# Norm additions and token sums moved from GpSimd to VectorE, first weights issued by SyncE, three g tiles in the first FFN

## The chip, the cores and the metric

The kernel runs on one core of a Trainium2 chip. The metric is the device time of one execution in microseconds. Engines go by the names of the profile: PE (TensorE matmul), PEld (its weight load), DVE (VectorE), ACT (ScalarE), POOL (GpSimd) and SP (SyncE, which here only issues DMA).

## The reference

Two transformer blocks on 1024 tokens of width 1024, one after the other, all in float32. Cut to the feed-forward parts, which the change touches:

```python
# first block
x = x + gt_m * rms_norm(y, g_post_mix)          # y: output of the first mixer
h = rms_norm(x, g_pre_ffn) * (1.0 + sc_f) + sh_f
up = dwconv3(h @ w_up, conv_w, conv_b)           # depthwise, width 3, over tokens
gate, val = jnp.split(up, 2, axis=-1)
y = (jax.nn.gelu(gate) * val) @ w_down
x = x + gt_f * rms_norm(y, g_post_ffn)
# second block
x = layernorm(A * x + 0.5 * swiglu(x, ffn1_w1, ffn1_w3, ffn1_w2), ln1_g, ln1_b)
x = layernorm(A * x + mixer(x), ln2_g, ln2_b)
x = layernorm(A * x + 0.5 * swiglu(x, ffn2_w1, ffn2_w3, ffn2_w2), ln3_g, ln3_b)
# swiglu(x, w1, w3, w2) = (silu(x @ w1) * (x @ w3)) @ w2, inner width 2816
```

## The kernel before

The stages follow each other: first mixer (it ends with `mixer1_out`), first FFN (`ffn1`), first `swiglu`, second mixer, second `swiglu`, and the last layer norm whose rows go to `out`. Each of the three FFNs has an up stage (`up`) and a down stage (`down`); of the time line, ffn1's up stage begins behind 517 us, its down tail ends near 1255, the first swiglu's up stage begins near 1297, the second's near 2502.

**Products.** A float32 product is made of three matmuls with operands split into a high and a low part: `split` (L103) lets ACT copy the high part (L87) and DVE subtract it from the source (L106); `mm3` (L108) issues high x high (L111), high x low (L112), low x high (L113). For the weights the names are raw (as loaded), wh and wl; for the tokens xh and xl.

**Up stage.** The inner width goes in 22 steps f of 128 columns; each takes the two weight matrices that belong together (gate and value) and the two halves of the tokens as a 2x2 by 2x2 block product, done with seven products P = 1 to 7 in the manner of Strassen, in the order 1, 2, 6, 7, 4, 5, 3, 12 matmuls of 512 columns each. P = 1 and 5 have their low weight part made by POOL (`POOL_LO`), the others by DVE; P = 6 and 4 need sums of weight blocks, made by POOL (L264, T<-raw). A load brings two f (128x8x256, 1 MB, L125). Loads issued by POOL are held in program order by `keep_in_program_order`; those on SP are not. PSUM banks (bA, bB) are added into `acc` tiles by DVE (L92).

**Token sums.** P = 7, 6 and 3 need sums of token blocks: s23 and s4, high and low. `cross_xt` (L208) makes them at the start of an up stage, for two pairs of token tiles in turn: four PE transposes into a PSUM bank per channel tile (L223), scale and shift to `acc` by ACT or DVE (`affine`, L98 and L205), then s4 and the sum for xh on POOL (L228, L231, L237), the two sums for s23 on DVE, and the splits.

**ffn1's glue** (L1675). When the gate's and the value's products are there (h[0], h[1], `acc` 0 and 1), ACT and DVE make the convolution (`conv`: ACT writes u at L1670, DVE adds two shifted terms with L101), ACT the gelu (L1683), DVE the product g * v. g is in `acc` tile 2 for even f and 4 for odd, v in 3 and 5. `left` (L383) then forms, for two f, the seven left operands of the down stage in place in the g tiles and stores them from SP to `gd` (L389): an even f stores half of g, an odd f stores its own g, combines with the even one's and stores that.

**Down stages and norms.** The tokens come in tiles of 128 rows in the order n = 0 to 7. In ffn1 `normed` (L1711) closes a pair of tiles: scale by the rms factor and gate, add the stored rows of the residual x1d (L1724), store to x2r. In the last layer norm, `ln_tail` with `last` (L660 to L679), ACT normalises (L673), then one multiply (L675) and one add (L677) per tile follow, split over POOL and DVE by tile.

**What sets the order.** A tile scheduler orders the instructions of each engine by priority and readiness; engines then run in order and wait by semaphores. `high_priority` raises the weights' preparation. `right` (L409) makes sums of w_down rows for ffn1's down stage during `mixer1_out`; its POOL work and DMAs are held in program order.

Of the kernel before, what the change touches and what calls it, by code (L numbers as in the profile page):

```python
# [13 lines left out]
OP = mybir.AluOpType  # L14
# [6 lines left out]
FF = 2816  # L21
# [17 lines left out]
class Kern:  # L39
# [168 lines left out]
    def cross_xt(self, pair, S23, S4, tmp, scale, bias):  # L208


        nc = self.nc
# [4 lines left out]
        r = lambda a: a.rearrange("p (t c) -> p t c", t=2)  # L216
        kept = lambda k: self.acc[:, o + k % 2, :].rearrange("p (i c) -> p i c", i=2)[:, :,
                                                                                      k // 2 * 256:k // 2 * 256 + 256]
        for k in range(4):
            ps = self.bankB([128, 2, 256])  # L220
            for i in range(2):
                for t in range(2):
                    nc.tensor.transpose(ps[:, i, t * 128:(t + 1) * 128], tiles[:, i, k, t, :], self.ident)  # L223
            hf = tiles[:, :, k]
            self.affine(hf, ps.rearrange("p i (t c) -> p i t c", t=2), k, k + 4, scale, bias, k % 2)
            a = kept(k)
            s4 = tmp[k]
            nc.gpsimd.tensor_tensor(out=r(s4), in0=r(a[:, 1]), in1=hf[:, 1], op=OP.subtract)  # L228
            self.tt(r(a[:, 0]), r(a[:, 0]), hf[:, 0], OP.subtract)
            self.tt(r(a[:, 1]), hf[:, 1], r(a[:, 0]), OP.subtract)  # L230
            nc.gpsimd.tensor_tensor(out=hf[:, 0], in0=hf[:, 0], in1=hf[:, 1], op=OP.add)  # L231
            self.split(S23[0][:, :, k, lc], S23[1][:, :, k, lc], a)
            x = [x[:, k::4, tk].rearrange("p i (t c) -> p i t c", t=2) for x in (self.xh, self.xl)]
            self.split(*x, hf)
        yield
        for k in range(4):
            nc.gpsimd.tensor_tensor(out=tmp[k], in0=tmp[k], in1=kept(k)[:, 0], op=OP.add)  # L237
            self.split(S4[0][:, k, lc], S4[1][:, k, lc], tmp[k])
        yield

    def up(self, pool, loads, h1, glue, scale, bias, gd, during=None, start=None, below=None):
# [112 lines left out]
        tmps = [spare[:, 2 + i // 2, i % 2 * 256:i % 2 * 256 + 256] for i in range(4)]  # L354
# [229 lines left out]
    def swiglu(self, w1, w3, w2, h1, ln, last, base, init, scale=None, bias=None, spill=None, during=None):  # L584
# [16 lines left out]
        with tc.tile_pool(name="up", bufs=1, reuse_waits="tile") as pool:  # L601
            self.up(pool, [lambda f, w=w: self.load_cols(w, f * 128, eng=nc.gpsimd) for w in (w1, w3)], h1, glue,
                    scale, bias, gd, during, below=(w2, td))
# [28 lines left out]
    def ln_tail(self, pool, ln, eps, last, bufs=5, rows=None):  # L632
# [3 lines left out]
        gb = []  # L636
# [1828 lines left out]
```

## Time and profile before

| | us |
|---|---|
| median of 3 runs | 3225.34 |
| lowest, highest | 3224.27, 3226.10 |
| the profiled execution | 3220.59 |
| its span in the trace | 3218.8 |
| mean granted PE clock | 0.953 |

The profile is of one execution. Its page gives the busy time of each engine and the costliest groups; the trace behind it answers for single stretches: busy time and granted clock by window, waits with what ended them, and a time line with every instruction's start, its duration, and in brackets the idle time before it with the releaser. PEclk is the granted clock as a share of full speed.

### The profile page before, as it was taken

The page shows a single profiled execution, that of the slowest core. Times are in us where ns is not written, and L with a number is a line of the kernel's source. Part 1 is how long each engine was busy: PE and PEld are TensorE (multiplying, and loading weights), DVE is VectorE, ACT ScalarE, POOL GpSimd, SP SyncE. Part 2 cuts the span into 40 slices and gives each one's busy share as a digit, 9 for nine tenths or more (in the row PEclk, how much of TensorE's full clock was granted, in tenths as well). Part 3 has the DMA queues.
Part 4 walks back from the last instruction along what each step waited for, and adds up shares of the span by engine and source line. Part 5 has one row for each costly group of instructions (what it writes and reads, how often), then busy time and mean ns, then how long its engine had stood idle before and what let it go on. Part 6 is the DMA issues. An engine that isn't in the chain of part 4 may idle for free. (4 is left out here: it accounts for less than half of the span.)

```text
span 3218.8 us, 38064 instructions
## 1 busy us (share of the span) xinstructions
PE 2932.0 (91%) x13810; PEld 2317.2 (72%) x13810; DVE 2368.8 (74%) x3855; ACT 1249.0 (39%) x2023; POOL 1168.6 (36%) x1001
## 2 busy tenths in 40 slices
PE   6899996799898999699999999977999799999996
PEld 4675565677777887578887888875677677887885
DVE  6982656887878656877776577799857887777567
ACT  5122532433333443323222443557762422222442
POOL 4422267655544002645553001131313655453003
PEclk9899998899999999799999999989999899999998
DMA  6116364222222673344444773110012265444762
GB/s 212 55 34 246 136 199 156 72 87 84 93 85 91 233 229 133 118 161 151 152 159 168 253 246 105 41 34 1 14 68 104 78 237 190 156 160 167 264 213 88
DMA packets 175508, 440.18 MB, mean 137 GB/s; under 512 B 16296, under 2 KB 36040, under 8 KB 175192
## 3 DMA queue, kind: packets, MB, share of 16 engines
q1 hardware_dynamic: 138924, 307.20, 27.4%
q0 software_dynamic: 36032, 130.19, 12.3%
q8 instruction: 109, 1.79, 0.2%
q14 instruction: 79, 0.65, 0.1%
q10 hardware_dynamic: 364, 0.35, 0.0%
HBM read 315.41 MB, written 122.27 MB: 136 GB/s over the span
## 5 line engine op out<-in xcount | busy, mean ns | idle before, releaser
L87 ACT ACTIVATE wh<-raw 128x512 fp32r<-128x512 f32 (+1 forms) x506 | 407.3, 826 | 839.6 <-PE bB L112 207.9
L106 DVE TENSOR_TENSOR wl<-raw,wh 128x1024 fp32r<-128x1024 f32 (+1 forms) x370 | 439.3, 1193 | 245.0 <-ACT wh L87 243.6
L111 PE MATMUL bB<-xh,wh 128*128 128x512 f32 (+1 forms) x860 | 343.3, 399 | 4.7 <-ACT xh L87 4.5
L112 PE MATMUL bB<-xl,wh 128*128 128x512 f32 (+1 forms) x860 | 340.3, 396 | 4.2 <-DVE xl L106 4.2
L113 PE MATMUL bB<-xh,wl 128*128 128x512 f32 (+1 forms) x860 | 339.5, 395 | 0.7 <-DVE wl L106 0.6
L92 DVE TENSOR_TENSOR acc<-acc 128x512 f32<-128x512 f32 (+2 forms) x306 | 306.7, 1015 | 19.6 <-DMA gdln_g<-acc 9.5
L106 POOL TENSOR_TENSOR wl<-raw,wh 128x512 fp32r<-128x512 f32 (+1 forms) x136 | 220.7, 1625 | 220.1 <-ACT wh L87 210.3
L111 PE MATMUL bA<-xh,wh 128*128 128x512 f32 (+1 forms) x508 | 211.4, 417 | 90.0 <-DVE acc L92 53.3
L264 POOL TENSOR_TENSOR T<-raw 128x512 f32<-128x512 f32 x132 | 200.1, 1516 | 182.9 <-DMA raw<-in_ffn_w 96.4
L92 DVE TENSOR_TENSOR acc<-bA,acc 128x512 f32<-128x512 f32 x226 | 150.4, 685 | 127.4 <-PE bA L113 127.1
L92 DVE TENSOR_TENSOR acc<-bB,acc 128x512 f32<-128x512 f32 x260 | 178.1, 686 | 69.2 <-PE bB L113 58.7
L264 POOL TENSOR_TENSOR T<-raw,T 128x512 f32<-128x512 f32 x66 | 106.8, 1619 | 309.4 <-DVE wl L106 307.0
L112 PE MATMUL bA<-xl,wh 128*128 128x512 f32 (+1 forms) x508 | 208.2, 411 | 1.0 <-DVE xl L106 1.0
L113 PE MATMUL bA<-xh,wl 128*128 128x512 f32 (+1 forms) x508 | 207.8, 409 | 0.2 <-DVE wl L106 0.2
L111 PEld LDWEIGHTS bB<-xh,wh 128*128 128x128 f32 x860 | 164.0, 191 | 46.8 <-ACT xh L87 6.0
L112 PEld LDWEIGHTS bB<-xl,wh 128*128 128x128 f32 x860 | 163.6, 190 | 44.6 <-DVE xl L106 5.9
L87 ACT ACTIVATE wh<-T 128x512 fp32r<-128x512 f32 x198 | 118.2, 624 | 191.9 <-PE bA L112 88.9
L113 PEld LDWEIGHTS bB<-xh,wl 128*128 128x128 f32 x860 | 163.4, 190 | 39.5 <-DVE wl L106 1.3
L111 PEld LDWEIGHTS bA<-xh,wh 128*128 128x128 f32 x508 | 101.5, 200 | 122.6 <-ACT wh L87 73.2
L101 DVE SCALAR_TENSOR_TENSOR acc<-acc,cw 128x1023 f32<-128x1023 f32 x88 | 138.6, 1576 | 62.2 <-ACT acc L1670 61.7
L111 PE MATMUL bA<-wh 128*128 128x512 f32 x432 | 170.5, 395 | 12.8 <-DVE acc L92 12.8
L112 PE MATMUL bA<-wl,wh 128*128 128x512 f32 x432 | 169.7, 393 | 0.0
(527 smaller groups left out, 7401.9 us busy)
## 6 DMA issues: line engine op xcount, KB each, us to landing
raw<-in_ffn_w POOLq DMA_DIRECT2D x44, 1024.0 KB, 6.1
raw<-gdln_g SPq DMA_DIRECT2D x70, 512.0 KB, 4.1
raw<-in_w_up POOLq DMA_DIRECT2D x22, 1024.0 KB, 6.2
tq<-in_ffn_w SPq DMA_DIRECT2D x44, 512.0 KB, 4.9
tdln_g<-tq SPq DMA_DIRECT2D x44, 512.0 KB, 2.6
gdln_g<-acc SPq DMA_DIRECT2D x44, 512.0 KB, 2.6
raw<-tdln_g SPq DMA_DIRECT2D x40, 512.0 KB, 5.0
raw<-gd SPq DMA_DIRECT2D x35, 512.0 KB, 4.0
```

Of the source, the lines that this page charges most:

```text
L87: self.nc.scalar.activation(out=out, in_=in_, func=AF.Copy)
L92: self.nc.vector.tensor_tensor(out=out, in0=a, in1=b, op=op)
L101: self.nc.vector.scalar_tensor_tensor(out=out, in0=a, scalar=s, in1=b, op0=op0, op1=op1)
L106: (eng or self.nc.vector).tensor_tensor(out=lo, in0=src, in1=hi.bitcast(F32), op=OP.subtract)
L111: mm(out, lhsT=wh, rhs=xh, start=start, stop=False)
L112: mm(out, lhsT=wh, rhs=xl, start=False, stop=False)
L113: mm(out, lhsT=wl, rhs=xh, start=False, stop=stop)
L264: sub = lambda o, a, b: nc.gpsimd.tensor_tensor(out=o, in0=a, in1=b, op=OP.subtract)
```

## The change

- `cross_xt` works on two channel tiles at a time (q = 0, 1). All sums are DVE operations of 512 elements (`self.tt`): ten per cross in place of eight DVE and twelve POOL operations of 256. The splits are grouped by q; the s4 temporaries are two of [128, 2, 256] in place of four of [128, 256].
- The loads of f = 0 in all three up stages are issued by SP (`eng=f and nc.gpsimd` gives 0, so the default) and no longer held in program order.
- In the last layer norm, and in ffn1's `normed`, all multiplies and adds are on DVE.
- In ffn1's glue g takes `acc` tiles 2, 3, 4 in turn by f % 3, and v is always tile 5.

```diff
@@ cross_xt
-        r = lambda a: a.rearrange("p (t c) -> p t c", t=2)
-        kept = lambda k: self.acc[:, o + k % 2, :].rearrange("p (i c) -> p i c", i=2)[:, :,
-                                                                                      k // 2 * 256:k // 2 * 256 + 256]
-        for k in range(4):
-            ps = self.bankB([128, 2, 256])
+        kept = self.acc[:, o:o + 2, :].rearrange("p j (i q c) -> p q j i c", i=2, q=2)
+        r = lambda a: a.rearrange("p j (t c) -> p j t c", t=2)
+        for q in range(2):
+            ks = slice(2 * q, 2 * q + 2)
+            for k in range(2 * q, 2 * q + 2):
+                ps = self.bankB([128, 2, 256])
+                for i in range(2):
+                    for t in range(2):
+                        nc.tensor.transpose(ps[:, i, t * 128:(t + 1) * 128], tiles[:, i, k, t, :], self.ident)
+                self.affine(tiles[:, :, k], ps.rearrange("p i (t c) -> p i t c", t=2), k, k + 4, scale, bias, k % 2)
+            a = kept[:, q]
+            h0, h1 = tiles[:, 0, ks], tiles[:, 1, ks]
+            self.tt(r(tmp[q]), r(a[:, :, 1]), h1, OP.subtract)
+            self.tt(r(a[:, :, 0]), r(a[:, :, 0]), h0, OP.subtract)
+            self.tt(r(a[:, :, 1]), h1, r(a[:, :, 0]), OP.subtract)
+            self.tt(h0, h0, h1, OP.add)
...
-            nc.gpsimd.tensor_tensor(out=r(s4), in0=r(a[:, 1]), in1=hf[:, 1], op=OP.subtract)
-            self.tt(r(a[:, 0]), r(a[:, 0]), hf[:, 0], OP.subtract)
-            self.tt(r(a[:, 1]), hf[:, 1], r(a[:, 0]), OP.subtract)
-            nc.gpsimd.tensor_tensor(out=hf[:, 0], in0=hf[:, 0], in1=hf[:, 1], op=OP.add)
...
-        for k in range(4):
-            nc.gpsimd.tensor_tensor(out=tmp[k], in0=tmp[k], in1=kept(k)[:, 0], op=OP.add)
-            self.split(S4[0][:, k, lc], S4[1][:, k, lc], tmp[k])
+        for q in range(2):
+            ks = slice(2 * q, 2 * q + 2)
+            self.tt(tmp[q], tmp[q], kept[:, q, :, 0], OP.add)
+            self.split(S4[0][:, ks, lc], S4[1][:, ks, lc], tmp[q])
@@ swiglu, and the same in ffn1
-            self.up(pool, [lambda f, w=w: self.load_cols(w, f * 128, eng=nc.gpsimd) for w in (w1, w3)], h1, glue,
+            self.up(pool, [lambda f, w=w: self.load_cols(w, f * 128, eng=f and nc.gpsimd) for w in (w1, w3)], h1, glue,
@@ ln_tail, last
-                    (nc.gpsimd if i - t + n in (0,2,5) else nc.vector).tensor_tensor(out=o[:, a], in0=o[:, a], in1=gb[0][:, a],
-                                                                      op=OP.mult)
-                    (nc.vector if m else nc.gpsimd).tensor_tensor(out=o[:, a], in0=o[:, a], in1=gb[1][:, a], op=OP.add)
+                    self.tt(o[:, a], o[:, a], gb[0][:, a], OP.mult)
+                    self.tt(o[:, a], o[:, a], gb[1][:, a], OP.add)
@@ ffn1, glue
-                o = 2 + f % 2 * 2
-                g, v = acc[:, o, :], acc[:, o + 1, :]
+                g, v = acc[:, 2 + f % 3, :], acc[:, 5, :]
@@ ffn1, normed
-                    (nc.vector if n > 5 else nc.gpsimd).tensor_tensor(out=a, in0=a, in1=x, op=OP.add)
+                    self.tt(a, a, x, OP.add)
```

The order of the instructions changes at the three starts of an up stage and in the two tails. (Behind the diff's lines in `cross_xt`, `ln_tail` and `ffn1` the line numbers of the changed kernel are 3, 2 and 1 higher.)

SP between the loads of w_out and ffn1, before (raw are the staging tiles, t the rows of the residual):

```order
L1600 DMA raw<-in_w_out 64x1024 x4
L1642 DMA x1d<-t_3070 128x1024
L1642 DMA x1d<-t_3157 128x1024
L1642 DMA x1d<-t_3265 128x1024
L1642 DMA x1d<-t_3352 128x1024
```

And SP at the same place in the changed kernel:

```order
L1602 DMA raw<-in_w_out 64x1024 x4
L125 DMA raw<-in_w_up 128x8x256 x2
L1644 DMA x1d<-t_3070 128x1024
L1644 DMA x1d<-t_3157 128x1024
L1644 DMA x1d<-t_3265 128x1024
```

The two first loads of w_up stand ahead of all eight stores of x1d.

POOL from the last sums of w_down rows (tq, td) to the first sums of weight blocks (T), before:

```order
L432 TENSOR_TENSOR tq<-tq 128x256 x4
L434 DMA td<-tq 128x2x256 x2
L125 DMA raw<-in_w_up 128x8x256 x2
L106 TENSOR_TENSOR wl<-raw,wh 128x512 x2
L228 TENSOR_TENSOR raw<-acc 128x256 x2
L231 TENSOR_TENSOR acc<-acc 128x2x128
L237 TENSOR_TENSOR raw<-raw,acc 128x256
L231 TENSOR_TENSOR acc<-acc 128x2x128
L237 TENSOR_TENSOR raw<-raw,acc 128x256
L228 TENSOR_TENSOR raw<-acc 128x256 x2
```

POOL there in the changed kernel:

```order
L435 TENSOR_TENSOR tq<-tq 128x256 x4
L437 DMA td<-tq 128x2x256 x2
L106 TENSOR_TENSOR wl<-raw,wh 128x512 x2
L267 TENSOR_TENSOR T<-raw 128x512
L267 TENSOR_TENSOR raw<-raw 128x4x128
L267 TENSOR_TENSOR T<-raw 128x512
L106 TENSOR_TENSOR wl<-raw,wh 128x512
```

The loads and the token sums are gone; the two low parts still stand behind the sums of w_down rows, and the weight sums follow at once. PE's order is the same in both: two matmuls of the first product, twelve transposes of token tiles, then the L113 that reads the first wl.

DVE in the last tail, ahead of the four additions of PSUM banks that let PE go on, before (rs_t and rstd belong to the rsqrt, t are output rows, lnr the gain or bias):

```order
L106 TENSOR_TENSOR wl<-raw,wh 128x1024
L92 TENSOR_TENSOR rs_t<-rstd 128x2
L92 TENSOR_TENSOR rs_t<-rs_t,rs_h 128x2
L101 SCALAR_TENSOR_TENSOR rstd<-rs_t,rstd 128x2
L101 SCALAR_TENSOR_TENSOR lnb<-mv,rstd 128x1
L675 TENSOR_TENSOR t_22743<-t_22743,lnr 128x1024
L101 SCALAR_TENSOR_TENSOR lnb<-mv,rstd 128x1
L106 TENSOR_TENSOR wl<-raw,wh 128x1024
L675 TENSOR_TENSOR t_22851<-t_22851,lnr 128x1024
L92 TENSOR_TENSOR acc<-bA,acc 128x512 x4
```

And DVE there in the changed kernel:

```order
L106 TENSOR_TENSOR wl<-raw,wh 128x1024
L92 TENSOR_TENSOR rs_t<-rstd 128x2
L92 TENSOR_TENSOR t_22652<-t_22652,lnr 128x1024
L92 TENSOR_TENSOR t_22659<-t_22659,lnr 128x1024
L92 TENSOR_TENSOR t_22652<-t_22652,lnr 128x1024
L92 TENSOR_TENSOR t_22659<-t_22659,lnr 128x1024
L92 TENSOR_TENSOR rs_t<-rs_t,rs_h 128x2
L92 TENSOR_TENSOR acc<-bA,acc 128x512 x4
```

Four operations on output rows now stand ahead of the four additions; one weight split, the end of the rsqrt and the two lnb have moved behind them. In ffn1's up stage the order on DVE is the same in both from about f = 4 on; there only the tiles of g and v differ.

## Rows read from the trace of the kernel before

**Rows 1.** Page, first part: busy us (share) xinstructions of each engine.

```profile
PE 2932.0 (91%) x13810; PEld 2317.2 (72%) x13810; DVE 2368.8 (74%) x3855; ACT 1249.0 (39%) x2023; POOL 1168.6 (36%) x1001
```

**Rows 2.** Stretches: us, busy of PE, PEld, DVE, ACT, POOL; PEclk, DMA, GB/s.

```profile
535.70:600.00 64.30, 37.73 (x177) 30.60 (x178) 53.23 (x82) 29.49 (x57) 42.51 (x39) 0.73 0.20 66
600.00:1060.00 460.00, 422.66 (x1738) 336.69 (x1737) 371.25 (x401) 165.54 (x228) 226.52 (x140) 0.96 0.27 94
658.00:662.00 4.00, 3.92 (x17) 3.21 (x18) 3.84 (x5) 1.24 (x1) 3.81 (x4) 1.00 0.61 193
792.00:796.00 4.00, 4.00 (x12) 3.12 (x11) 2.37 (x3) 1.16 (x1) 3.81 (x3) 0.57 0.68 220
836.60:881.20 44.60, 40.87 (x168) 32.55 (x168) 35.75 (x39) 15.71 (x22) 22.58 (x15) 0.96 0.26 89
1297.00:1352.00 55.00, 40.81 (x164) 32.38 (x163) 52.72 (x64) 23.16 (x50) 44.16 (x40) 0.72 0.22 76
1450.00:1900.00 450.00, 448.01 (x1936) 363.22 (x1935) 315.43 (x377) 152.53 (x218) 150.58 (x110) 1.00 0.54 183
2502.00:2560.00 58.00, 41.21 (x198) 34.14 (x197) 57.02 (x81) 27.72 (x53) 40.85 (x37) 0.79 0.23 78
```

**Rows 3.** Waits of PE, 480 to 600: line <- releaser, us, times, longest.

```profile
PE bA L111 <- ACT wh L87: 28.5, 2, 26.5
```

**Rows 4.** Time line at ffn1's start: start, us, instruction, [idle before].

```profile
543.64 0.80 PE L111 MATMUL bA<-xh,wh 128*128 128x512 f32 x1 [26.52 <-ACT wh L87]
...
547.99 0.78 PE L113 MATMUL bA<-xh,wl 128*128 128x512 f32 x1
...
535.72 1.80 POOL L125 DMA_DIRECT2D raw<-in_w_up  x2
...
445.81 72.67 SPq L1642 DMA_DIRECT2D x1d<-t  x7
```

**Rows 5.** Waits of PE and of DVE, 600 to 1060.

```profile
PE bA L111 <- DVE acc L92: 37.3, 11, 4.6
...
DVE acc L101 <- ACT acc L1670: 60.4, 35, 4.0
```

**Rows 6.** Time line of DVE, then ACT, 853 to 893 (two f of ffn1).

```profile
853.28 2.52 DVE L92 TENSOR_TENSOR acc<-acc 128x512 f32<-128x512 f32 x3
...
862.32 2.20 DVE L101 SCALAR_TENSOR_TENSOR acc<-acc,cw 128x1023 f32<-128x1023 f32 x1 [3.56 <-ACT acc L1670]
...
871.15 1.28 DVE L101 SCALAR_TENSOR_TENSOR acc<-acc,cw 128x1023 f32<-128x1023 f32 x1 [1.31 <-ACT acc L1670]
...
875.86 1.21 DVE L92 TENSOR_TENSOR acc<-acc 128x1024 f32<-128x1024 f32 x1
...
861.05 1.24 ACT L1670 ACTIVATE acc<-acc,cw 128x1024 f32<-128x1024 f32 x1 [4.86 <-DMA gd<-acc]
...
890.43 1.24 ACT L1670 ACTIVATE acc<-acc,cw 128x1024 f32<-128x1024 f32 x1
```

**Rows 7.** Groups by form, 546 to 600: xcount, busy, mean ns, idle.

```profile
L228 POOL TENSOR_TENSOR raw<-acc 128x256 f32<-128x256 f32 x8 | 7.9, 995 | 2.2 <-DVE acc L98 2.2
...
L92 DVE TENSOR_TENSOR acc<-acc 128x256 f32<-128x256 f32 x16 | 10.4, 682 | 0.3 <-ACT acc L205 0.3
```

**Rows 8.** Waits of PE: 1225-1296, 1296-1380, 2502-2580, 3140-3219, in this order.

```profile
PE bA L111 <- DVE acc L92: 5.7, 2, 3.9
...
PE bA L111 <- ACT wh L87: 8.0, 1, 8.0
...
PE bA L111 <- ACT wh L87: 4.6, 1, 4.6
...
PE bA L111 <- DVE acc L92: 10.0, 2, 8.9
```

**Rows 9.** Time line of DVE in the last tail.

```profile
3153.12 2.38 DVE L92 TENSOR_TENSOR rs_t<-rstd 128x2 f32<-128x2 f32 x1
...
3166.24 2.47 DVE L92 TENSOR_TENSOR acc<-bA,acc 128x512 f32<-128x512 f32 x4
```

More of the change, by code (lines that the diff above doesn't have):

```diff
@@ L215, in cross_xt @@
         tiles = self.acc[:, 2 * pair:2 * pair + 2, :].rearrange("p t (i k c) -> p i k t c", i=2, k=4)
-        r = lambda a: a.rearrange("p (t c) -> p t c", t=2)
-        kept = lambda k: self.acc[:, o + k % 2, :].rearrange("p (i c) -> p i c", i=2)[:, :,
-                                                                                      k // 2 * 256:k // 2 * 256 + 256]
-        for k in range(4):
-            ps = self.bankB([128, 2, 256])
-            for i in range(2):
[L222 to L227, printed above, removed]
-            nc.gpsimd.tensor_tensor(out=r(s4), in0=r(a[:, 1]), in1=hf[:, 1], op=OP.subtract)
-            self.tt(r(a[:, 0]), r(a[:, 0]), hf[:, 0], OP.subtract)
-            self.tt(r(a[:, 1]), hf[:, 1], r(a[:, 0]), OP.subtract)
-            nc.gpsimd.tensor_tensor(out=hf[:, 0], in0=hf[:, 0], in1=hf[:, 1], op=OP.add)
-            self.split(S23[0][:, :, k, lc], S23[1][:, :, k, lc], a)
-            x = [x[:, k::4, tk].rearrange("p i (t c) -> p i t c", t=2) for x in (self.xh, self.xl)]
-            self.split(*x, hf)
@@ new lines, in cross_xt @@
+        kept = self.acc[:, o:o + 2, :].rearrange("p j (i q c) -> p q j i c", i=2, q=2)
[14 more added lines that the diff above has]
+            self.tt(h0, h0, h1, OP.add)
+            for i in range(2):
+                self.split(S23[0][:, i, ks, lc], S23[1][:, i, ks, lc], a[:, :, i])
+                x = [x[:, 4 * i + 2 * q:4 * i + 2 * q + 2, tk].rearrange("p j (t c) -> p j t c", t=2)
+                     for x in (self.xh, self.xl)]
+                self.split(*x, tiles[:, i, ks])
@@ L353, in up @@
             prep(*seq[s])
-        tmps = [spare[:, 2 + i // 2, i % 2 * 256:i % 2 * 256 + 256] for i in range(4)]
+        tmps = [spare[:, 2 + q, :].rearrange("p (j c) -> p j c", j=2) for q in range(2)]
         cross = [self.cross_xt(2 * (1 - h1) + i, S23, S4, tmps, scale, bias) for i in range(2)]
@@ L1690, in start @@
                 self.copy(cw[0], ps.rearrange("p a b -> p (a b)"))
-            self.up(pool, [lambda f, o=o: self.load_cols(wu, o + f * 128, eng=nc.gpsimd) for o in (0, FF)], 0, glue,
+            self.up(pool, [lambda f, o=o: self.load_cols(wu, o + f * 128, eng=f and nc.gpsimd) for o in (0, FF)], 0, glue,
                     self.gs_f, self.sh_f, gd, start=start)
```

## The prediction

> **What bounds the kernel now.** I read the page's busy shares first, then the table of stretches, then the waits of each stretch, and for each wait the time line around it. The reader is to see that TensorE is the bound and where it is not fed. PE is busy 91% of 3218.8 us, DVE 74%, POOL 36% [rows 1]; so a change that touches only DVE, POOL and SP can pay only where PE waits for them. The table of stretches shows where [rows 2]. In the first swiglu's up stage (1450 to 1900) PE issues 1936 matmuls in 450 us, 0.2324 us each, at granted clock 1.00: nothing to gain. In the up stage of ffn1 (600 to 1060) 1738 matmuls take 460 us; at 0.2324 they would take 404, so 56 us are lost. The waits of PE there are 37.3 us, 11 times, all for a DVE line that adds a PSUM bank into acc [rows 5]. The rest, 0.04 x 460 = 18 us, is the clock (mean 0.96). What the clock does behind a wait is in the rows too: after the 1.33 us wait at 658 the next 4 us stand at 1.00, after the 2.8 us wait at 791 they stand at 0.57, between the two levels of 1.2 and 2.4 GHz [rows 2]. The other losses are the three starts of an up stage (granted clock 0.73, 0.72 and 0.79 [rows 2]) and the two tails, each with waits of its own [rows 3, 8].
>
> **The first weights (SP for POOL).** PE waits 26.5 us before its first ffn1 matmul at 543.64 [rows 3, 4]. The chain behind it: POOL works off the w_down row sums that are pinned ahead, issues the two 1 MB loads at 535.72, they land about 6 us later, ACT converts, PE starts [rows 4]. SP in the changed kernel has the two loads behind the w_out loads and ahead of all x1d stores; the first x1d store goes out at 445.81 [rows 4], so the weights lie ready some 70 us before 517, when mixer1_out's last matmul ends. What is queued behind them on SP are the x1d stores, whose reader is the down stage 700 us later; price nothing. What is late next: the low parts of P = 1 are POOL work (two L106) and still stand behind the row sums. They ran at 542.6 behind the ACT conversion; now they can begin at 535.72, and PE's first L113, which waits for them, moves from 547.99 [rows 4] to about 537.2 (535.72 plus one of 1.48): 10.8 us, the lower bound. But PE's order puts the first twelve token transposes ahead of that L113, so that the cross chain on DVE starts near 523 and not at 546. The waits behind the start (6.8 us at 569.4 for s23l, 3.5 at 582.4 for acc, and six smaller ones of 6 us together, by the same view as [rows 3]) lie on that chain. If all of them go, 10.8 + 16.3 = 27 us is the upper bound. By the chain s23l is done near 550, about when the 48 early matmuls end (537.2 + 48 x 0.2324 = 548.4 and some clock), against 569.4 before: 18 us, and a little of the later ones. **I take 20.** For the first swiglu the same edit works on the 8.0 us wait at 1296.5 [rows 8]: POOL issues its loads at 1286.3, behind two norm adds, and PE has been idle for most of the time when they land. For the second swiglu the loads were already in time; the edit is worth nothing there.
>
> **Token sums (cross_xt) on DVE.** Per cross 12 POOL operations of 128x256, 1.0 us each, go [rows 7]; two crosses at each of three starts make 72. DVE had 8 of 256 elements at 0.68 [rows 7], 5.5 us, and gets 10 of 512. A 512 operation of this kind costs 0.84 in the steady stage (three in 2.52 [rows 6]), so 8.4 us per cross: 3 more than before. The ends are 6.1, at half of the 1.21 us that 1024 elements take [rows 6], and 10, were each as slow as the POOL operation that it replaces. Against that, DVE work next to POOL is stretched: an operation on 128x2, 0.16 us where POOL is idle, took 2.38 beside a POOL add [rows 9]. Over the first start I count 20 us of stretch (each operation against the shortest of its form) in 51 us of DVE, with 38 us of POOL work; removing 23 us of that POOL work should take 11 to 12 of the stretch away. Net about 5 us less DVE per start, and POOL reaches its weight sums (L264) earlier by the 12 us that the cross sums took. In the first start this is inside the 20. In the swiglu1 start PE waits 8.0 [rows 8], then 4.9, 3.4 and 7.4 at 1315, 1331 and 1373, and runs 55 us at 0.72 [rows 2]. I take all of the 8.0, a third of the other three (5) and 2 of clock: **15** (8 to 22). In swiglu2 the waits are 4.6 [rows 8], 4.6, 4.3, 2.4 and 2.4 at clock 0.79 [rows 2]; a third of them and 1 of clock: **7** (0 to 12).
>
> **Three g tiles.** In the period of two f from 836.6 to 881.2 PE issues 168 matmuls (39.0 us at 0.2324) in 44.6 us, DVE is busy 35.75 [rows 2]. At 853.28 DVE makes the three combinations of an odd f, SP stores them; at 861.05 ACT starts the convolution of the next even f after 4.86 us of waiting for a store gd<-acc, since it writes the same tile; DVE stands 3.56 us behind it at 862.32 [rows 6]; its evictions come late, and PE waits 3.7 us at the end of the period. DVE waits for that convolution 60.4 us in 35 times, 4.0 at the longest [rows 5]. With three tiles the store has a whole f more. What stays of the 3.56 is the usual 1.31 that DVE waits for ACT's convolution [rows 6]: 2.25 direct. The rest follows only if PE's leftover wait is short enough for the clock to stay, as behind the 1.33 us wait [rows 2]. DVE is late next: 35.75 busy + its own waits for ACT (four, 0.71 and 3 x 1.31) and for a store (0.36) = 40.75 per two f, above PE's 39.0. So 44.6 (the mean distance of the waits is 45.4) goes to about 40.8, 4.2 less, ten times in the stage: **42**. Bounds: 2.25 x 10 = 23, and all 56. The v tile becomes a single one; its product ends at 877.07 and the next v convolution starts at 890.43 [rows 6], 13 us apart, so it costs nothing.
>
> **Norm tails.** In ffn1's down tail four POOL adds of 2.4 to 3.4 us stretch DVE and PE waits 5.7 us, 3.9 of it at once [rows 8]. DVE gets them at 1.2 each; with the clock behind it, **5** (0 to 8). In the final tail PE waits 8.9 of 10.0 us at 3167.66 [rows 8] for four evictions that DVE reaches at 3166.24 [rows 9]. From 3153.12 on DVE spends 13.1 us ahead of them, of which rs_t 2.38, rstd 2.26, wl 2.53 and a multiply 3.36 are held by POOL. The new order has a 0.16, four of 1.2 and another 0.16 there: 5.2 us, so the evictions run by 3158.4, when PE's bank is ready. 7.5, and 2 of clock. Behind PE's end three small operations held for 5.6 us lose the hold, two or three adds of 1.2 come in, and the last one should end some 3.5 sooner. **13** (6 to 16).
>
> **Sum.** 20 + 42 + 5 + 15 + 7 + 13 = 102 on the profiled execution's 3220.59; it stands 4.75 below the median of the runs, 3225.34, so I carry the difference over to the median: 3225.34 - 102 = **3123**. All lower bounds (10.8 + 8 + 0 + 23 + 0 + 6 = 48) give 3177, all upper ones (27 + 22 + 12 + 56 + 8 + 16 = 141) 3084.
>
> **Rivals.** (a) *The g tiles give only the direct part.* DVE, at 40.75 of a possible 44.6, has a second wait behind the first, PE's leftover stays over 2 us and the clock falls each time. For: DVE has 371 us of work in 460 [rows 2], ordered by hand-set priorities. Against: 1.3 us waits keep the clock. Gain 23 for 42: 3142. (b) *DVE holds the starts.* The ten moved sums per cross meet POOL's weight sums, which now begin at the same time, and each waits for a whole one, 1.3 to 1.7 us. POOL has 42.5 - 23 = 19 us left in the first start [rows 2, 7], which caps the price at 19 per start. The 128x2 operation that took 2.38 [rows 9], as long as a POOL add of 1024 elements in that tail (2.40), speaks for such a hold; that the cross sums on DVE already ran beside POOL before, at 0.68 each [rows 7], speaks against a full one. Held to the cap it eats the 15 and 7 and half of the 20: 3155. The Trainium skill, page "SBUF — State Buffer", section "SBUF: two separate sides", has a rule for it: VectorE and GpSimd share a pair of ports under an exclusive lock, and a VectorE operation with two SBUF inputs that meets a GpSimd operation is held until that one ends. By that rule the trace agrees for the 128x2 operation, and all the moved sums are of the held kind, which would make (b) the outcome; the forecast goes by the 0.84 of the rows. (c) *The upper end*: PE runs through ffn1 at 0.2324 and the first start loses every wait: 102 + 14 + 7 = 123, 3102 or less. (d) *Slower*: the single v tile. If ACT's v convolution had to wait for the product of the f before, DVE, ACT and PE would run in turn in each of 22 f. With the 42 gone, 60 us of other gains remain, so it decides from 60 / 22 = 2.7 us per f; at 4 us per f the time is 3225 - 60 + 88 = 3253. The 13 us of slack speak against it. (e) *It doesn't do what it says*: SP's loads wait for staging tiles until the end of mixer1_out and hold the x1d stores; then the first start gives nothing more than POOL's relief (8): 3135, still inside (a).
>
> **How the numbers follow.** Forecast, 3103 to 3141: 0.62, (e) within it. (a), 3142 to 3155: 0.13. (b) 0.09. (c) 0.11. (d) 0.03. Everything cancels: 0.02. The range 3092 to 3165 leaves out (d), the cancelled case, a part of (b) and the far end of (c). A measurement of this kernel can tell about 0.2%, 6.5 us, from no change; faster by more 0.95, within it 0.02, slower by more 0.03.
>
> **What would show it.** In the profile after: no ACT wait for gd<-acc in ffn1 and PE waits there under 2 us with the clock at 1.00; if the waits stay over 2.5 us with the clock falling, the g step is wrong as (a). The first L113 of ffn1 near 537 and the wait for s23l gone; the wait before the first matmul of swiglu1 gone. DVE operations on 128x2 at 0.16 in the tails. 128x512 sums above 1.3 us in the starts would show (b); an ACT wait for a DVE product in front of each v convolution would show (d).

## The result and the profile after

The changed kernel takes 3133.1 us (median of 4 runs, 3131.9 to 3135.9), the kernel before 3224.8 in the runs beside it: 0.9723 of the time, 95% interval 0.9703 to 0.9743, that is 89 us less by this ratio and 92 by the medians. The forecast was 3123. The profiled execution after took 3134.06 us with a span of 3132.3; against the profiled one before (span 3218.8) 86.5 us less. What follows is read on that pair.

Where they went can be read from the start of the same matmul in both traces (below: "by the same matmuls"). A difference with a minus means that the changed kernel is ahead there.

| place (time before, us) | difference there | gained in the stretch | forecast |
|---|---|---|---|
| end of mixer1_out (516) | +3.5 | | |
| behind ffn1's start (600) | -11.5 | 15.0 | 20 |
| ffn1 up, 600 to 700 | -10.1 | -1.4 | } 42 |
| ffn1 up, 700 to 1060 | -43.2 | 33.1 | } |
| ffn1's down tail (1256) | -49.8 | 6.6 | 5 |
| swiglu1's start (1400) | -66.3 | 16.5 | 15 |
| second mixer (2500) | -65.4 | -0.9 | |
| swiglu2's start (2700) | -71.2 | 5.8 | 7 |
| last tail (3175) | -80.7 | 9.5 | 9.5 |
| end of the span (3218.8) | -86.5 | 5.8 | 3.5 |

The 3.5 us ahead of the first changed instruction are no work of the change: 2.2 of them stand already at 400, before SP's new loads at 421, and the run of the third experiment, the same kernel up to there, stands at -1.7 at 516; the fifth, there the kernel before, stands at +3.3. So the stretches of the change gained 90.0, where the forecast had 102.

The page's first part, after: PE is busy 15 us less than before [rows 1] with the same 13810 matmuls, as its mean granted clock is 0.966 and was 0.953, and has 93% of a shorter span; POOL lost 115 us and 94 instructions.

```profile
PE 2917.2 (93%) x13810; PEld 2306.4 (74%) x13810; DVE 2333.0 (74%) x3871; ACT 1247.9 (40%) x2011; POOL 1053.4 (34%) x907
```

The stretches of after (columns as in [rows 2]): ffn1's up stage, three places of it, one period of two f, two places outside it, the starts of swiglu1 and swiglu2, and the last tail.

```profile
588.50:1016.70 428.20, 410.20 (x1739) 327.09 (x1738) 373.95 (x399) 166.91 (x227) 221.11 (x138) 0.99 0.29 100
...
649.50:653.50 4.00, 4.00 (x11) 3.15 (x12) 3.29 (x4) 1.72 (x2) 3.00 (x3) 0.62 0.28 38
732.30:736.30 4.00, 4.00 (x17) 3.25 (x18) 3.28 (x4) 1.25 (x1) 3.90 (x4) 1.00 0.66 224
935.30:939.30 4.00, 4.00 (x18) 3.23 (x19) 3.28 (x4) 1.24 (x1) 3.81 (x4) 1.00 0.69 226
...
691.50:732.30 40.80, 39.47 (x169) 31.52 (x169) 35.62 (x39) 15.92 (x22) 22.03 (x15) 1.00 0.28 97
...
522.50:526.50 4.00, 4.00 (x20) 3.29 (x21) 3.79 (x12) 3.99 (x8) 3.06 (x5) 0.71 0.51 161
1658.70:1662.70 4.00, 4.00 (x18) 3.23 (x19) 2.69 (x4) 1.16 (x2) 3.29 (x4) 1.00 0.33 131
...
1240.00:1296.00 56.00, 42.45 (x192) 34.71 (x193) 49.95 (x80) 25.37 (x48) 23.44 (x16) 0.85 0.30 104
...
2436.00:2494.00 58.00, 47.32 (x238) 39.56 (x237) 50.99 (x87) 29.31 (x54) 26.03 (x17) 0.88 0.31 100
3069.00:3101.00 32.00, 31.53 (x139) 25.81 (x138) 27.83 (x60) 11.96 (x11) 0.00 (x0) 1.00 0.39 141
```

The matmuls of ffn1's up stage that took 460 us (1738 records, [rows 2]) take 428 (1739). A period of two f is 40.8 us and DVE has the same 35.6 us of work in it as before (35.75 in 44.6). In the last tail PE is fed to the end of the down products: it is busy 31.5 of 32 us. The starts of swiglu1 and swiglu2 stand at a clock of 0.85 and 0.88 (0.72 and 0.79 before [rows 2]). In the middle of swiglu1 the difference stays at -66.3 for 500 us. In ffn1's up stage the clock follows the waits as it did before: behind 2.70 us of waiting at 649.5 the next 4 us stand at 0.62, behind 1.32 at 732.3 and 1.70 at 935.2 at 1.00.

The waits of PE and of DVE in ffn1's up stage of after, 590 to 1020:

```profile
PE bA L111 <- DVE acc L92: 15.9, 10, 5.0
...
DVE acc L101 <- ACT acc L1672: 40.2, 36, 1.3
```

Against [rows 5]: DVE's wait for ACT's convolution fell from 60.4 to 40.2, the longest from 4.0 to 1.3, the usual length that the prediction set aside. ACT has no wait for a store of gd left. Of PE's 15.9 us, 5.0 are at 602 and 2.7 at 649; from 690 on none is over 1.7.

### The profile page after: what moved, and what is told of

Its sections match the earlier page's. It is cut to its first block, busy times and chain, and to the rows that moved or that the text cites. A ratio compares the mean times of both kernels' runs of the same rounds, so it can differ in the third digit from the quotient of the medians.

```text
span 3132.3 us, 37952 instructions
## 1 busy us (share of the span) xinstructions
PE 2917.2 (93%) x13810; PEld 2306.4 (74%) x13810; DVE 2333.0 (74%) x3871; ACT 1247.9 (40%) x2011; POOL 1053.4 (34%) x907
## 4 chain that ended last, share of the span: by engine, by line
PE 50%; DVE 12%; ACT 3%; issue 2%; POOL 2%; DMA 2%; SPq 0%; DVEq 0%; POOLq 0%; ACTq 0%
PE bB L112 8%; PE bB L111 8%; PE bB L113 8%; PE bA L111 7%; PE bA L112 6%; PE bA L113 6%; DVE acc L92 3%; DVE wx L2072 1%; PE bB L2268 1%; DVE wl L106 1%; PE bB L2252 1%; DMA raw<-in_ffn_w 1%; POOL T L267 1%; ACT junk L2086 1%; PE bA L2219 1%
## 5 line engine op out<-in xcount | busy, mean ns | idle before, releaser
L106 DVE TENSOR_TENSOR wl<-raw,wh 128x1024 fp32r<-128x1024 f32 (+1 forms) x370 | 427.7, 1161 | 212.4 <-ACT wh L87 211.4
L106 POOL TENSOR_TENSOR wl<-raw,wh 128x512 fp32r<-128x512 f32 (+1 forms) x136 | 227.9, 1680 | 449.8 <-ACT wh L87 426.8
L113 PE MATMUL bB<-xh,wl 128*128 128x512 f32 (+1 forms) x860 | 340.6, 396 | 13.0 <-POOL wl L106 12.3
L92 DVE TENSOR_TENSOR acc<-acc 128x512 f32<-128x512 f32 (+1 forms) x294 | 304.5, 1047 | 15.0 <-DMA gdln_g<-acc 8.4
L113 PE MATMUL bA<-xh,wl 128*128 128x512 f32 (+1 forms) x508 | 203.8, 401 | 0.0
L113 PEld LDWEIGHTS bB<-xh,wl 128*128 128x128 f32 x860 | 164.0, 191 | 52.3 <-POOL wl L106 12.9
L112 PEld LDWEIGHTS bB<-xl,wh 128*128 128x128 f32 x860 | 164.2, 191 | 40.1 <-issue 1.2
L106 DVE TENSOR_TENSOR wl<-T,wh 128x512 fp32r<-128x512 f32 x198 | 149.3, 778 | 28.7 <-ACT wh L87 28.3
L113 PE MATMUL bA<-wh,wl 128*128 128x512 f32 x432 | 168.2, 389 | 0.0
```

The lines of the kernel that those rows point to most:

```text
L92: self.nc.vector.tensor_tensor(out=out, in0=a, in1=b, op=op)
L106: (eng or self.nc.vector).tensor_tensor(out=lo, in0=src, in1=hi.bitcast(F32), op=OP.subtract)
L112: mm(out, lhsT=wh, rhs=xl, start=False, stop=False)
L113: mm(out, lhsT=wl, rhs=xh, start=False, stop=stop)
```

## Experiments

Each was timed beside the kernel before, and the ratio with its 95% interval is to that; the medians are compared with the changed kernel's 3133.1. Stretches by the same matmuls are read on the profiled executions and, but for the fifth experiment, named by the changed kernel's times.

**1. Two g tiles again.**

```diff
-                g, v = acc[:, 2 + f % 3, :], acc[:, 5, :]
+                g, v = acc[:, 2 + f % 2 * 2, :], acc[:, 3 + f % 2 * 2, :]
```

> The changed kernel with g back on two tiles (acc 2 and 4) and v on 3 and 5; all else as changed. Theory: in the changed kernel's trace the period of two f in ffn1 is 40.1 to 41.1 us from 691 on, against 45.4 before, over the 8 periods in which ACT waited for a store of gd. With two tiles the wait returns in all of them: 8 x 4.2 = 33 us, so about 3166 against 3133, PE waits of 3 to 4.6 us each 45 us apart and the clock below 1.00 behind them. Rival: the stage went faster because the starts and the tails left DVE less behind; then the tile itself is worth only the direct part, 2.25 x 8 = 18 us (3151), with waits about 2 us and the clock kept.

3179.3 us, 0.9855 (0.9833 to 0.9878) of before: 46 more by the median, 39.7 by the profiled pair, of which 37.7 lie between 608 and 1017 of ffn1 and nothing elsewhere. The waits in its up stage (PE, ACT, 590 to 1070):

```profile
PE bA L111 <- DVE acc L92: 41.8, 11, 5.1
...
ACT acc L1672 <- DMA gd<-acc: 45.1, 9, 7.5
```

The store's wait is back, PE waits 3.8 to 5.1 us every 45 us from 695 on. The rival, in which the other parts carry the stage, is out.

**2. First loads on POOL again.**

```diff
-eng=f and nc.gpsimd
+eng=nc.gpsimd
```

> The changed kernel with the first loads of all three up stages back on POOL, in program order. Theory: in ffn1 the loads go out behind the row sums near 538 and land near 545, as before; but the second low part on POOL was not done before 540 in the changed kernel either, and the token sums chain ran only behind it, so the loss is only the difference of the two, about 8 us: near 3141. In the first swiglu POOL has no norm adds ahead of the loads any more, so they are in time and the wait before the first matmul does not come back. Rival: the loads on SP carry the whole gain of both starts, 15 + 8 us: near 3156, with the 8 us wait back at the first swiglu.

3147.3 us, 0.9757 (0.9732 to 0.9781): 14 more. By the same matmuls all of it stands at ffn1's start, from -2.3 at 516 to +13.7 at 608; what follows adds up to 3 and loses it again. PE's waits at ffn1's start, 505 to 600, and two places of DVE's time line there:

```profile
PE bA L111 <- ACT wh L87: 30.9, 2, 29.4
...
551.20 0.54 DVE L98 TENSOR_SCALAR acc<-bB,gs_f,sh_f 128x256 f32<-128x256 f32 x1 [0.60 <-ACT acc L205]
...
569.50 1.29 DVE L106 TENSOR_TENSOR s23l<-acc,s23h 128x512 fp32r<-128x512 f32 x2
```

The place is as expected, the 8 us was too little. What it left out: here all of DVE's chain from the token tiles to s23l, 18.3 us, runs behind the first product (551.20 to 569.50). In the changed kernel a first part of it ran from 524.6 to 536.0, and only 10.5 us stood behind the late product (545.98 to 556.47, shown with the sixth experiment). At the first swiglu PE's longest wait before the steady part is 3.5 us, and that start loses 1.4.

**3. Token sums as before.** `cross_xt` and its four temporaries from the kernel before, all else as changed.

> The changed kernel with the token sums as before: per channel tile of 256 elements, twelve of them on POOL. Theory: POOL work beside DVE stretches DVE and delays the weight sums; the three starts lose some 5 (ffn1), 8 (first swiglu) and 5 us (second): near 3150, and the DVE operations of 128x256 in the starts are at 0.6 to 0.7 us each instead of 0.34. Rival: the moved sums are held by POOL's weight sums as long as they save; then it is within 5 us of 3133.

3148.7 us, 0.9763 (0.9742 to 0.9783): 15.6 more. The profiled pair, 16.3 apart, has 7 at ffn1's start (from -5.2 at 516 to +1.8), 5.6 at swiglu1's and 9 at swiglu2's. Groups by form at swiglu1's start, of this kernel (1240 to 1300) and then of the changed one (1235 to 1290):

```profile
L92 DVE TENSOR_TENSOR acc<-acc 128x256 f32<-128x256 f32 x16 | 10.6, 675 | 0.0
L106 DVE TENSOR_TENSOR s23l<-acc,s23h 128x512 fp32r<-128x512 f32 x8 | 9.5, 1218 | 0.0
```

```profile
L92 DVE TENSOR_TENSOR acc<-acc 128x512 f32<-128x512 f32 x12 | 7.9, 676 | 0.0
...
L106 DVE TENSOR_TENSOR s23l<-acc,s23h 128x512 fp32r<-128x512 f32 x8 | 5.4, 675 | 0.0
...
L92 DVE TENSOR_TENSOR raw<-raw,acc 128x512 f32<-128x512 f32 x4 | 4.8, 1217 | 0.0
...
L92 DVE TENSOR_TENSOR raw<-acc 128x512 f32<-128x512 f32 x4 | 2.7, 677 | 0.0
...
L92 DVE TENSOR_TENSOR rs_t<-rs_y 128x2 f32<-128x2 f32 x3 | 0.4, 145 | 0.0
```

Sixteen operations of 256 elements beside POOL's 24 took 10.6 us. The changed kernel has twenty of 512 for all of them: sixteen at 0.68, and four (raw<-raw,acc) at 1.22 in the mean, together 15.4 us. So all of POOL's sums cost DVE 4.8 us in two crosses. DVE gets more than that back in its other work: the same eight s23l splits took 9.5 us and take 5.4, and the operations on 128x2 are at 0.145. Counted as the prediction counts stretch (each operation against the shortest of its form), DVE's stretch in this start is about 24 us here, 22 in the kernel before and 10 in the changed one.

The mean of 1.22 hides two kinds. DVE and POOL of the changed kernel at one of the four:

```profile
1263.12 1.76 DVE L92 TENSOR_TENSOR raw<-raw,acc 128x512 f32<-128x512 f32 x1
...
1262.72 1.61 POOL L267 TENSOR_TENSOR raw<-raw 128x512 f32<-128x512 f32 x1
```

Two of the four met a POOL weight sum and took 1.76 and 1.75, the other two 0.68. Over the three starts, 54 of the 60 moved sums took 0.63 to 0.69; six took 0.97 to 1.77, and each of these ended 0.54 to 0.55 us behind the end of a POOL operation that it met. So the hold of rival (b) of the prediction is there, but few of the moved sums meet it: it costs 4.8 us over the three starts, where (b) had up to 19 per start. The rival of this experiment, in which the hold eats the gain, is out.

**4. Tails on POOL again.** The four lines of `ln_tail` and `normed` as before.

> The changed kernel with the multiplies and adds of the last layer norm and the adds of ffn1's norm split over POOL and DVE as before. Theory: the last tail loses its 16 us and ffn1's down tail 6.6 us: near 3155, with the 8.9 us wait of PE back in the last tail. The first swiglu's start loses nothing, since SP issues its loads. Rival: the adds on DVE only moved the hold elsewhere, and the loss is under 10 us (3143).

3157.3 us, 0.979 (0.9769 to 0.9811): 24 more; 6.1 at ffn1's down tail, 10.1 in the last tail and 5.5 behind PE's end. Time line of DVE in its last tail, with the POOL operation that the first line meets:

```profile
3090.23 2.36 DVE L92 TENSOR_TENSOR rs_t<-rstd 128x2 f32<-128x2 f32 x1
...
3090.03 2.55 POOL L678 TENSOR_TENSOR t<-t,lnr 128x1024 f32<-128x1024 f32 x1 [159.32 <-ACT t L676]
...
3100.05 3.36 DVE L678 TENSOR_TENSOR t<-t,lnr 128x1024 f32<-128x1024 f32 x1
3103.33 2.47 DVE L92 TENSOR_TENSOR acc<-bA,acc 128x512 f32<-128x512 f32 x4
```

and of the changed kernel at the same place:

```profile
3082.54 0.15 DVE L92 TENSOR_TENSOR rs_t<-rstd 128x2 f32<-128x2 f32 x1
3082.61 4.62 DVE L92 TENSOR_TENSOR t<-t,lnr 128x1024 f32<-128x1024 f32 x4
3087.16 0.15 DVE L92 TENSOR_TENSOR rs_t<-rs_t,rs_h 128x2 f32<-128x2 f32 x1
3087.23 2.48 DVE L92 TENSOR_TENSOR acc<-bA,acc 128x512 f32<-128x512 f32 x4
```

With POOL's adds DVE needs 13.1 us from rs_t to the four additions, without them 4.7, although four operations of 1024 stand between, where the first has three (two multiplies and a weight split). The hold of [rows 9] is seen again: the 128x2 operation ends at 3092.59, POOL's multiply at 3092.58.

**5. Three g tiles alone,** on the kernel before.

> The kernel before with only the g tiles changed: three in turn, v always tile 5. Theory: the tile is worth the same without the other parts. In the first experiment the up stage of ffn1 lost 37.7 us when the third tile went; so 38 us less than before, near 3187, eight long waits of PE gone, the period of two f 40 to 41 us. Rival: part of those 38 us needs DVE relieved at the start by the other parts; then the first periods keep their waits and it gives 18 to 25 us (3200 to 3207).

3189.3 us, 0.989 (0.9861 to 0.9918) of before. By the same matmuls it has +0.4 against the kernel before at 700 and -32.6 at 1060: 33 us, and nothing elsewhere. The tile needs no other part of the change; the first 100 us of the stage gain nothing in either kernel.

**6. First low parts on DVE** (for P = 1 of f = 0 and 1 of ffn1).

```diff
-                self.split(h, l, src, nc.gpsimd if P in POOL_LO else None)
+                self.split(h, l, src, nc.gpsimd if P in POOL_LO and not (start and (f, P) in early[:2]) else None)
```

> The changed kernel with the low parts of the first two weight products of ffn1 (P = 1 of f = 0 and 1) made by DVE and not by POOL behind the row sums. Theory: the 12.3 us wait of PE at 540 for POOL's wl goes, and with it the 16.1 us in which ACT stood for that product's bank ahead of the token sums; what bounds next are POOL's weight sums, which still begin near 539. Gain 8 to 12 us: near 3123. Rival: the token chain and the weight sums bound the start anyway, the wait only moves to the s23 products: gain under 4 us (3130).

3127.1 us, 0.9699 (0.9672 to 0.9727): 6 less than the changed kernel by the medians, 4.2 at ffn1's start by the profiled pair (from -0.8 at 516 to -5.0 at 608). The intervals of the two ratios overlap, so the 6 us rest on the medians and on this stretch. The time line of the changed kernel shows what it takes away (PE, POOL, ACT, DVE, SP at ffn1's start):

```profile
522.50 0.50 PE L111 MATMUL bA<-xh,wh 128*128 128x512 f32 x1 [1.84 <-ACT wh L87]
...
540.17 0.80 PE L113 MATMUL bB<-xh,wl 128*128 128x512 f32 x1 [12.29 <-POOL wl L106]
...
538.85 2.50 POOL L106 TENSOR_TENSOR wl<-raw,wh 128x512 fp32r<-128x512 f32 x2
...
544.83 0.60 ACT L87 ACTIVATE raw<-bB 128x512 f32<-128x512 f32 x1 [16.10 <-PE bB L113]
...
524.58 0.54 DVE L98 TENSOR_SCALAR acc<-bB,gs_f,sh_f 128x256 f32<-128x256 f32 x1
...
545.98 0.69 DVE L106 TENSOR_TENSOR xl<-acc,xh 128x512 fp32r<-128x512 f32 x1 [9.93 <-ACT xh L87]
...
556.47 1.29 DVE L106 TENSOR_TENSOR s23l<-acc,s23h 128x512 fp32r<-128x512 f32 x2
...
421.00 9.65 SPq L125 DMA_DIRECT2D raw<-in_w_up  x2
```

and that of the sixth kernel what comes in its place (PE, ACT, POOL, DVE):

```profile
548.38 0.58 PE L111 MATMUL bA<-s23h,wh 128*128 128x256 f32 x1 [8.89 <-ACT wh L87]
552.51 0.58 PE L112 MATMUL bA<-s23l,wh 128*128 128x256 f32 x1 [3.55 <-DVE s23l L106]
...
546.14 0.63 ACT L87 ACTIVATE xh<-acc 128x512 fp32r<-128x512 f32 x1 [6.85 <-DVE acc L92]
...
540.13 1.27 POOL L267 TENSOR_TENSOR T<-raw 128x512 f32<-128x512 f32 x1
...
539.18 2.77 DVE L92 TENSOR_TENSOR acc<-acc 128x512 f32<-128x512 f32 x1
```

PE did up to 12.8 us earlier what stood behind the 12.3 us wait, and gave 8.1 of it back before the first s23 product. That new wait is not for POOL's weight sums themselves, which are done at 544.8: ACT, which makes the high part of its weights, stands 6.85 us for DVE's token sums, one of which took 2.77 us beside POOL. The result lies between theory and rival: the wait was real, and most of it was cover for the token sums.

**7. Token sums on DVE by single channel tiles** (256 elements, 20 operations per cross).

> The changed kernel with the token sums on DVE, but per channel tile of 256 elements as before (20 DVE operations per cross, none on POOL). Theory: that POOL is out of the way is what pays, not the pairing; 20 operations of about 0.4 us cost 8 us per cross against 6.8 for ten of 0.68, so it is within 5 us of the changed kernel (3133 to 3138). Rival: pairing pays half of the 15.6 us that the token sums are worth; then near 3141.

3133.5 us, 0.9722 (0.9689 to 0.9754), the changed kernel's time within the error. (The profiled execution was this kernel's slowest, 3144.6; the others were 3130.8 to 3135.7.) What pays is that POOL is out of the sums; taking two channel tiles at a time is worth nothing that the times can tell. By the same matmuls that slowest execution loses 2.1 us at swiglu1's start and 5.0 at swiglu2's; whether that is the price of the single tiles or of the one execution stays open, and the interval reaches up to the rival's 3141.

**8. A shorter shifted term.**

```diff
-                self.stt(u[:, :-1], h[:, 1:], cw[0][:, 88 + j:89 + j], u[:, :-1], OP.mult, OP.add)
+                self.stt(u[:, :n], h[:, 1:n + 1], cw[0][:, 88 + j:89 + j], u[:, :n], OP.mult, OP.add)
-                    conv(v, h[1], NF + f)
+                    conv(v, h[1], NF + f, 64)
```

> The changed kernel with the second shifted term of the value's convolution in ffn1 added for 64 tokens in place of 1023 (so the other tokens lack that term): DVE loses about 1.1 us per f and nothing else changes. Theory: in the changed kernel DVE bounds the period of two f (40.7 us, of it 35.6 busy and the rest its waits for ACT), PE needs 39.0; so the period goes to 39.0 to 39.5 and the stage loses 10 to 13 us: near 3121. Rival: the period is set by the chain from PE's bank over DVE and ACT back to PE and not by DVE's amount of work: under 4 us (3130 or more).

3119.1 us, 0.967 (0.9638 to 0.9702): 14 less, 12.0 of them in ffn1's up stage (608 to 1017). A stretch of 300 us in it, and the same stretch of the changed kernel below:

```profile
700.00:1000.00 300.00, 299.50 (x1281) 240.05 (x1280) 258.31 (x292) 119.33 (x165) 153.06 (x99) 1.00 0.31 105
```

```profile
700.00:1000.00 300.00, 291.85 (x1244) 232.84 (x1243) 261.31 (x283) 117.94 (x163) 159.37 (x100) 1.00 0.28 97
```

Per f (84 matmuls) DVE is busy 16.9 us and not 17.6, 0.7 less where 1.1 was expected, and PE is fed without a gap (299.5 of 300). So in the changed kernel DVE bounds this stage, by its work and its waits for ACT together: 87% busy, yet late. The edit takes the operation out of DVE's work and out of the chain over ACT and DVE alike, so these two are not told apart.

**9 and 10. The last one or two blocks of w_down rows on DVE,** on top of the sixth.

```diff
-        vec, dma = (nc.gpsimd, nc.gpsimd) if small else (nc.vector, nc.sync)
+        vec, dma = (nc.vector if q >= 10 else nc.gpsimd, nc.gpsimd) if small else (nc.vector, nc.sync)
...
```

The tenth has q >= 9. On DVE the subtractions are no longer held in program order.

> The kernel of the sixth experiment (first low parts on DVE), and the eight subtractions of the last block of w_down rows, pinned on POOL ahead of ffn1's weight sums, made by DVE. Theory: there POOL's weight sums began at 540.1, behind the row sums, and DVE was stretched beside them until 548 (a subtraction of 512 elements took 2.77 us); with 8 us of POOL work gone from 528 to 539 the weight sums begin near 532 and the 8.9 us wait of PE before the first s23 product shrinks: 5 to 8 us less, near 3121. Rival: what bounds there is the chain of the token sums on DVE, which now gets 3 to 5 us of subtractions more; then it is within 3 us of 3127.

> The same with the last two blocks of w_down rows on DVE (16 subtractions). Theory: a further 8 us of POOL work gone from 512 to 523; POOL is ahead of DVE by then, so at most 3 us less than with one block, near 3119. Rival: as for one block; DVE gets 6 to 10 us more in the tail of mixer1_out and it is 3 to 6 us more than with one.

3148.8 and 3147.2 us, 0.9759 (0.9742 to 0.9775) and 0.9756 (0.9741 to 0.977), about 21 more than the sixth. Neither side of what was asked decided it. The subtractions were placed on DVE ahead of the residual addition that empties mixer1_out's bank, and their load is issued by POOL at 522 only; the time line of the ninth (PE, then DVE):

```profile
538.98 0.77 PE L1636 MATMUL bA<-wh,xh 128*128 128x512 f32 x1 [28.94 <-DVE t L101]
...
525.60 0.42 DVE L435 TENSOR_TENSOR tq<-tq 128x256 f32<-128x256 f32 x1 [27.67 <-DMA tq<-in_w_down]
```

An in-order engine stood 27.7 us (27.6 in the tenth) in front of work that was ready.

**11. First loads and ffn1's norm adds on POOL.** Parts of the second and the fourth together.

> The changed kernel with two parts undone at once: the first loads back on POOL and ffn1's norm adds back on POOL. Alone, the loads cost 14 us, all at ffn1's start and nothing at the first swiglu, the adds (with the last tail) 6 us at ffn1's down tail. Theory: at the first swiglu either part alone lets the loads go out in time, and only both together bring the 8 us wait back: 14 + 6 + 8 = 28, near 3161. Rival: the wait there went for another reason (the token sums): 20, near 3153, and no wait of PE over 3 us before the first swiglu matmul.

3162.8 us, 0.9806 (0.9791 to 0.982): 29.7 more. PE's longest wait, 1215 to 1300:

```profile
PE bA L111 <- ACT wh L87: 8.2, 1, 8.2
```

The wait before the first swiglu product is back, with 11.7 us at that start by the same matmuls, though neither part alone brought it (1.4 and -0.7). Either edit removes it: SP in front, or POOL free to issue.

**12. The ninth with the order forced.** The subtractions held behind the last residual addition, their stores on SP.

```diff
-                self.right(pool, A["w_down"][0], self.td, 3 + t, 256, 2)()
+                rows = self.right(pool, A["w_down"][0], self.td, 3 + t, 256, 2)
+                if t < 7:
+                    rows()
...
             self.flush(99)
+            rows()
```

> The ninth experiment again with the eight subtractions of the last block of w_down rows held on DVE behind the last residual addition (in the ninth they stood ahead of it and DVE waited 27.7 us for their load), their stores on SP. So on DVE they come directly ahead of the s23l splits, and POOL goes from its last load straight to ffn1's weight sums. Theory: POOL's weight sums begin near 527 and not 540, DVE is not stretched beside POOL's subtractions from 528 to 539, the 8.9 us wait before the first s23 product shrinks to 2 to 4: 5 us less than the sixth experiment, near 3122. Rival: the token sums on DVE bound the start; the 3.4 us of subtractions ahead of s23l take back what POOL's absence gives, and it is within 3 us of 3127.

3126.9 us, 0.9692 (0.9679 to 0.9705), the sixth's time. POOL, PE and DVE at ffn1's start:

```profile
530.45 1.30 POOL L267 TENSOR_TENSOR T<-raw 128x512 f32<-128x512 f32 x1
...
545.59 0.58 PE L111 MATMUL bA<-s23h,wh 128*128 128x256 f32 x1 [4.37 <-ACT wh L87]
553.15 0.58 PE L112 MATMUL bA<-s23l,wh 128*128 128x256 f32 x1 [6.98 <-DVE s23l L106]
...
548.99 3.51 DVE L435 TENSOR_TENSOR tq<-tq 128x256 f32<-128x256 f32 x8
552.41 1.28 DVE L106 TENSOR_TENSOR s23l<-acc,s23h 128x512 fp32r<-128x512 f32 x2
```

The weight sums begin at 530 and not at 540, DVE comes through its token sums to 549, 2.8 us sooner, and the 3.5 us of subtractions take it back: PE's wait before the first s23 product falls from 8.89 to 4.37 us, the one for s23l rises from 3.55 to 6.98. This is as the rival has it: past the low parts, DVE's chain of the last tokens' norm and sums bounds ffn1's start.

The sixth and the twelfth are the fastest complete versions, 6 us below the changed kernel by the medians; the intervals of their ratios still touch that of the changed kernel.

## Why the prediction was right, and where its terms were off

The direction and the six places were right, and the sum (102) stands 10 us above the medians' 92 and 12 above the 90 that the stretches gained. The two largest terms were too high, three of the others a little too low.

**Three g tiles, 42 forecast, 33 measured** behind 700 (31.7 in the whole stage). The mechanism and the length of the new period were right: forecast 40.75 us for two f, set by DVE; measured from 691 to 975: 40.8, 40.5, 40.4, 40.8, 40.1, 41.1, 40.1. Experiment 8 shows that DVE is what is late, experiment 1 that the store's wait was the cause. What failed is the factor "ten times in the stage". I divided 460 us by the period, though the waits of that stage were there to be counted: from 701 to 1018 eight long ones, while those at 658 and 679 were 1.3 and 1.1 us and cost nothing. The seven periods between these eight were 45.2 us in the mean, not 45.4, and became 40.55: 4.6 less each, not 4.2, and 32.4 together. So the count was the error (ten for seven), and the gain per period, taken too small, hid a part of it. (The stage's 56 us also held the wait at 612, which belongs to the start and is still there, 5.0 at 602.) Undoing the tile in the changed kernel cost 37.7, doing it alone gave 33; with it undone the period is 45.6 (695 to 1014) against 45.2 before (702 to 1018), and what makes the rest of the difference stays open.

**ffn1's start, 20 forecast, 15 measured;** 16 came back with the loads undone and 7 with the token sums undone, so the two overlap. The loads went out at 421, and PE began at 522.5. The step that failed is "the cross chain on DVE starts near 523" and is done near 550. It did start (524.6), but from 536.0 on it stood 9.9 us behind ACT, and ACT 16.1 us behind PE: ACT's next instruction was the copy of the second product's bank, and that product waited for POOL's low part until 540. I had followed POOL's late low part to PE, and the token sums to DVE, but not through ACT's queue, where one is ahead of the other. The low part came at 538.85, not 535.7; 3 us of this go with the late mixer1_out of the profiled run. The first L113, which I had put at 537, ran at 525: its low part is made by DVE (it is of P = 2), and the one made by POOL is that of the second product. s23l ended at 560, and not 550.

**Token sums.** The cost was right: 7.7 us per cross, where 8.4 was taken and 5.3 had been. So was the stretch that goes with POOL's work: 11 to 12 us forecast per start, 21 us before and 10 after at ffn1's start, 22 and 10 at swiglu1's.

**Norm tails, 5 and 13 forecast; 6.6 and 15.3 measured,** with 6.1 and 15.6 when they were undone. The working held: 4.7 us of DVE where 5.2 were forecast, and the small operations behind PE's end lose their hold.

**swiglu1, 15 forecast, 16.5 measured.** The size was right, its split was not: I put the 8.0 us on the first loads. In the changed kernel they are worth 1.4 there (experiment 2), because POOL, without the adds, would issue them in time; only both undone bring the wait back, with 11.7 us at that start (experiment 11). The token sums account for 5.6.

**swiglu2, 7 forecast, 5.8 measured;** undoing the token sums cost 9 there. The starts still wait in other places: 6.5 us at 2472 for ACT, 5.1 at 2503 for DVE.

**The rivals.** (a) would have left waits over 2 us with the clock falling; from 690 on they are at most 1.7 and the clock stays. (b) had as its sign 128x512 sums above 1.3 us in the starts. Four of the 60 were (1.40 to 1.77), so the mechanism is there and only its size was small (experiment 3). The 0.68 of [rows 7] that the prediction set against it is a mean as well: seven of those sixteen took 0.41 or 0.42, two about 0.5, and seven 0.94 to 1.26. The rule of the Trainium skill that stood with (b) ("SBUF — State Buffer", "SBUF: two separate sides": of a VectorE operation with two SBUF inputs and a GpSimd operation that reads SBUF, the one that comes second is held until the other ends) agrees with the six held sums and with the 128x2 operation of experiment 4, which ended 0.01 us behind POOL's. It did not make (b) the outcome, since what POOL has left in the starts meets few of the moved sums. (d): ACT's waits for DVE ahead of the convolutions are ended by additions of PSUM banks, none by the product g * v. (e): SP's loads went out 28 us ahead of the first x1d store.

## What to carry to other kernels

Count the waits that an edit removes in the rows, and do not multiply one period by the length of the stage: a stall of a pattern need not be there in every turn. When a chain of steps is said to run while an engine waits, follow each step through the queue of every in-order engine it visits, ACT's too: what stands ahead of it there may be waiting for the very thing that is late. Two edits that remove the same wait cannot be priced each by itself; undo them singly and together.

## What the runs showed that was not expected

The price of a neighbour lies in single meetings, and a mean hides it. A DVE sum of 512 elements took 0.68 us by itself and up to 1.77 when it met a POOL operation, and whatever it took, it ended 0.54 to 0.55 us behind that operation. One of 256 elements takes 0.41 by itself; the 0.675 of experiment 3 is the mean of ten at 0.41 or 0.42 and six of 0.90 to 1.48. DVE of the seventh kernel, 1240 to 1295:

```profile
L92 DVE TENSOR_TENSOR raw<-raw,acc 128x256 f32<-128x256 f32 x8 | 3.0, 408 | 0.0
```

And in ffn1's up stage the clock took waits of PE of up to 1.7 us without falling (1.00 behind 1.32 and 1.70, and in the kernel before behind 1.33), while behind 2.70 us it stood at 0.62 for the next 4 us. So there the eight waits of 4.0 us in the mean, cut to 1.1, gave back 4.6 us per period and not only 2.9. The length of a wait does not settle it elsewhere: behind 1.84 us at 522.5 the next 4 us stand at 0.71, behind 2.04 us at 1658.7 at 1.00.
